# Add and RMS norm over 65,536 rows: the 2-row tile moved from last to first, and the last tile moved in pieces

## The chip, the cores and the metric

The kernel runs on one core of one Trainium2 chip. Times are microseconds (us) of the whole program on the device. One execution at a time was profiled; its page and its trace are what is read below. The profile's span is about 2 us shorter than the measured time of the same execution (3736.0 against 3738.2 for the kernel before); spans are compared with spans and times with times.

## The reference

```python
def setup_inputs():
    batch, seq, dim = 32, 2048, 2048
    return {"x": randn(batch, seq, dim), "residual": randn(batch, seq, dim),
            "gamma": np.ones(dim), "eps": np.float32(1e-6)}        # all float32

def reference(x, residual, gamma, eps):
    z = x + residual
    rms = np.sqrt(np.mean(z ** 2, axis=-1, keepdims=True) + eps)
    return (z / rms * gamma).astype(np.float32)
```

There are 65,536 rows of 2048 floats. Two such arrays are read and one is written, 1610.6 MB together, and each value is used once. Little can be saved by computing faster if the transfers fill the time.

## The kernel before

A tile is 128 partitions times R = 6 rows, 6.29 MB. 65,536 rows are 85 full tiles and one of 2 rows. There are three slots for z (which holds x, then the sum, then the result) and one slot for the residual.

```python
    R = 6
    NZ = 3
    sizes = [R] * n_full + ([left] if left else [])       # 85 x 6 rows, then 2 rows
    ...
    def load_x(i):
        nc.sync.dma_start(out=z_slots[i % NZ][:, : sizes[i], :], in_=rows(x_f, i))
    def load_r(i):
        nc.sync.dma_start(out=r_slot[:, : sizes[i], :], in_=rows(r_f, i))
    def store(i):
        nc.sync.dma_start(out=rows(o_f, i), in_=z_slots[i % NZ][:, : sizes[i], :])

    def compute(i):
        z = z_slots[i % NZ]
        groups = [(a, min(a + 3, sizes[i])) for a in range(0, sizes[i], 3)]
        for a, b in groups:
            # DVE: z += r over three rows; ACT: Square with a running sum, row by row; ACT: Sqrt
            ...
        for (a, b), rms in zip(groups, rms_of):
            # DVE: reciprocal, then z * rstd * gamma, row by row
            ...

    load_x(0)
    load_r(0)
    load_gamma()
    load_x(1)
    compute(0)
    load_r(1)
    for i in range(1, n_tiles):
        store(i - 1)
        if i + 1 < n_tiles:
            load_x(i + 1)
        compute(i)
        if i + 1 < n_tiles:
            load_r(i + 1)
    store(n_tiles - 1)
```

All these transfers are issued by SyncE (SP), in this order, and each waits there for its slot. A full tile's store therefore waits for all its scalings, and the next x load stands behind that store. The residual load of tile i+1 waits for the adds of tile i.

## Time and profile before

| | before |
|---|---|
| time, median of 3 runs | 3736.8 us (3736.49 to 3737.15) |
| DVE, ACT busy | 62%, 29% of the span |
| data moved | 1610.83 MB, mean 431 GB/s |
| rate between 100 and 3690 us | 433 GB/s |

These lines are from the page of the kernel before: the engines' busy time, the DMA share and rate in 40 slices, and the DMA queues (packets, MB, share of the 16 engines' time).

```profile
span 3736.0 us, 2707 instructions
DVE 2311.6 (62%) x858; ACT 1078.6 (29%) x1197; POOL 0.2 (0%) x4
DMA  9999999999999999999999999999999999999998
q1 hardware_dynamic: 37152, 1610.63, 99.7%
q14 instruction: 20, 0.16, 0.0%
```

The DMA engines are busy in every slice, and no other engine is near it. The Trainium skill, "DMA: Bandwidth & Descriptors", section "Where 436 GB/s comes from", puts the ceiling of the sixteen ports at 435.2 GB/s; the trace's 433 agrees with that. So the middle of the kernel has no slack, and what can be won lies at the start and at the end.

The windows view of the kernel before shows the holes. Its columns are the stretch, its length, busy time (and instructions) of DVE, ACT and POOL, the clock, the DMA share and GB/s.

```profile
46.00:48.00 2.00, 0.72 (x2) 1.97 (x5) 0.00 (x0) 1.00 1.07 320
48.00:50.00 2.00, 1.97 (x2) 1.97 (x3) 0.00 (x0) 1.00 0.33 123
76.00:78.00 2.00, 1.97 (x3) 1.90 (x4) 0.00 (x0) 1.00 0.43 147
100.00:3690.00 3590.00, 2220.04 (x821) 1034.05 (x1148) 0.00 (x0) 1.00 1.00 433
3702.00:3714.00 12.00, 11.96 (x7) 4.46 (x7) 0.00 (x0) 1.00 0.13 55
```

The timeline of the kernel before says what the holes waited for: start, duration, engine, line and operation; SPq lines are transfers being issued.

```profile
46.58 0.33 SPq L66 DMA_DIRECT2D r_slot<-in_residual_dram  x1
61.94 0.35 SPq L69 DMA_DIRECT2D out_dram<-z  x1
3693.68 0.33 SPq L66 DMA_DIRECT2D r_slot<-in_residual_dram  x1
3707.33 6.88 DVE L98 SCALAR_TENSOR_TENSOR z<-z,rstd,gamma_tile 128x2048 f32<-128x2048 f32 x3
3714.12 4.41 DVE L76 TENSOR_TENSOR z<-z,r_slot 128x4096 f32<-128x4096 f32 x1
3714.23 13.92 SPq L69 DMA_DIRECT2D out_dram<-z  x2
```

The second residual's load is issued at 46.58, when the three loads before it have drained. At the end the 2-row residual is loaded (from 3693.68, landed on the slowest engine by 3711.4) before the last full tile's scalings end at 3714.2; its store can't go out earlier, and nothing else is queued.

One more thing can be read from the trace. Every transfer is spread over the sixteen DMA engines, and each engine reports when its share has landed. Sorting these sixteen times of one transfer shows how far the engines stand apart. In the kernel before, the last full x or r transfers have twelve engines within 1.1 us, and four late ones: 3.5, 6.8, 7.2 and 9.3 us behind the first. At the start the sixteen lie within 1.7 us.

### The profile page before, as it was taken

What the parts mean: (1) busy time and instruction counts of PE and PEld (TensorE: products, weight loads), DVE (VectorE), ACT (ScalarE), POOL (GpSimd) and SP (SyncE); (2) the same over time, 40 slices, a digit from 0 to 9 for tenths busy, and PEclk for the clock granted to TensorE, in tenths of its full rate; (3) what the DMA queues carried; (4) which work ended last, traced back from release to release, by engine and by line L of the source; (5) the groups of instructions that cost most, each with busy time, mean ns of one, the idle gap of its engine ahead of it and who ended that gap; (6) DMA issues with size and microseconds to landing.
All of it is one profiled execution on the core that took longest, in us unless ns stands there. A gap on an engine that the chain in (4) does not pass through costs nothing.

```text
span 3736.0 us, 2707 instructions
## 1 busy us (share of the span) xinstructions
DVE 2311.6 (62%) x858; ACT 1078.6 (29%) x1197; POOL 0.2 (0%) x4
## 2 busy tenths in 40 slices
DVE  6555666665566666556666655666665566666556
ACT  2222233222223322222332222233222223322223
POOL 0000000000000000000000000000000000000000
DMA  9999999999999999999999999999999999999998
GB/s 410 429 432 434 433 434 432 435 433 434 433 434 433 433 434 434 433 435 432 434 433 434 434 434 433 434 432 435 432 436 432 435 432 435 433 434 433 435 432 369
DMA packets 37180, 1610.83 MB, mean 431 GB/s; under 512 B 4132, under 2 KB 4132, under 8 KB 4132
## 3 DMA queue, kind: packets, MB, share of 16 engines
q1 hardware_dynamic: 37152, 1610.63, 99.7%
q14 instruction: 20, 0.16, 0.0%
q10 hardware_dynamic: 8, 0.03, 0.0%
HBM read 1073.77 MB, written 536.87 MB: 431 GB/s over the span
## 4 chain that ended last, share of the span: by engine, by line
DMA 70%; DVE 30%; issue 0%; ACT 0%; DVEq 0%; SPq 0%
DMA r_slot<-in_residual_dram 70%; DVE z L76 30%; DVE z L98 0%; ACT sq_junk L79 0%; DVE rstd L96 0%; DVEq L160 0%; DVEq L76 0%; SPq L63 0%; ACT rms L86 0%
## 5 line engine op out<-in xcount | busy, mean ns | idle before, releaser
L76 DVE TENSOR_TENSOR z<-z,r_slot 128x6144 f32<-128x6144 f32 x171 | 1111.7, 6542 | 1385.4 <-DMA r_slot<-in_residual_dram 1385.4
L79 ACT ACTIVATE sq_junk<-z 128x2048 f32<-128x2048 f32 x512 | 963.5, 1882 | 2620.0 <-DVE z L76 2603.5
L98 DVE SCALAR_TENSOR_TENSOR z<-z,rstd,gamma_tile 128x2048 f32<-128x2048 f32 x512 | 1173.6, 2347 | 6.0
L79 ACT ACTIVATION_READ_ACCUMULATOR sq_junk<-z 128x1 f32 x512 | 95.5, 186 | 0.0
L86 ACT ACTIVATE rms<-ssq,eps_tile 128x3 f32<-128x3 f32 x171 | 50.7, 296 | 5.5
L96 DVE RECIPROCAL rstd<-rms 128x3 f32<-128x3 f32 x171 | 29.5, 172 | 5.7 <-ACT rms L86 5.7
L114 DVE LOAD_MASK_SELECT gamma_tile<-gamma_tile x1 | 0.0, 14 | 17.8 <-DMA gamma_tile<-in_gamma_dram 17.8
L79 ACT ACT_TABLE_LOAD x1 | 1.3, 1283 | 18.8 <-DMA z<-in_x_dram 18.8
L114 DVE STREAM_SHUFFLE gamma_tile<-gamma_tile 128x2048 f32<-128x2048 f32 x1 | 2.4, 2418 | 0.0
L109 DVE MEMSET gamma_tile<- 128x2048 f32 x1 | 1.8, 1765 | 0.4 <-issue 0.4
L86 ACT ACT_TABLE_LOAD x1 | 1.3, 1283 | 0.0
L60 DVE MEMSET eps_tile<- 128x1 f32 x1 | 0.1, 59 | 0.8 <-PEq L146 0.8
L146 POOL MEMSET const-bfloat16-1.0<- 128x1 bf16 x1 | 0.1, 101 | 0.0
L146 POOL MEMSET const-uint8-127<- 128x1 uint8 x1 | 0.1, 101 | 0.0
L146 POOL MEMSET const-float32-0.0<- 128x1 f32 x1 | 0.1, 98 | 0.2 <-issue 0.2
L146 POOL MEMSET const-float32-1.0<- 128x1 f32 x1 | 0.1, 98 | 0.0
## 6 DMA issues: line engine op xcount, KB each, us to landing
z<-in_x_dram SPq DMA_DIRECT2D x85, 6144.0 KB, 45.0
r_slot<-in_residual_dram SPq DMA_DIRECT2D x85, 6144.0 KB, 30.4
out_dram<-z SPq DMA_DIRECT2D x85, 6144.0 KB, 30.9
z<-in_x_dram SPq DMA_DIRECT2D x1, 2048.0 KB
r_slot<-in_residual_dram SPq DMA_DIRECT2D x1, 2048.0 KB
out_dram<-z SPq DMA_DIRECT2D x1, 2048.0 KB, 7.3
gamma_tile<-in_gamma_dram ACTq DMA_DIRECT2D x4, 8.0 KB
```

What stands on the lines that cost most here:

```text
L60: nc.vector.memset(eps_tile, float(eps))
L76: nc.vector.tensor_add(out=z[:, a:b, :], in0=z[:, a:b, :], in1=r_slot[:, a:b, :])
L79: nc.scalar.activation(out=sq_junk, in_=z[:, g, :], func=Act.Square, accum_out=ssq[:, g - a : g - a + 1],)
L86: nc.scalar.activation(out=rms[:, : b - a], in_=ssq[:, : b - a], func=Act.Sqrt, bias=eps_tile, scale=inv_d,)
L96: nc.vector.reciprocal(out=rstd[:, : b - a], in_=rms[:, : b - a])
L98: nc.vector.scalar_tensor_tensor(out=z[:, g, :], in0=z[:, g, :], scalar=rstd[:, g - a : g - a + 1], in1=gamma_tile, op0=mult, op1=mult,)
L109: nc.vector.memset(gamma_tile, 0.0)
L114: nc.vector.stream_shuffle(gamma_tile, gamma_tile, [0] * 32)
L146: nc = _bacc.Bacc("TRN2", target_bir_lowering=False, num_devices=1)
```

## The change

The intent: put the 2-row tile first, so that the first store comes early; hold its residual in the third z slot, which is free then, so that the next residual can be queued at once; and move the last tile's residual and result in 2-row pieces, so that its computation hides behind the store of the tile before.

```diff
-    sizes = [R] * n_full + ([left] if left else [])
+    sizes = ([left] if left else []) + [R] * n_full
 ...
-    stats = ctx.enter_context(tc.tile_pool(name="stats", bufs=3))
+    stats = ctx.enter_context(tc.tile_pool(name="stats", bufs=6))
 ...
+    last = n_tiles - 1
+    piece = 2
+
+    def pieces(i):
+        k = sizes[i]
+        return [(a, min(a + piece, k)) for a in range(0, k, piece)] if i == last else [(0, k)]
+
+    def r_of(i):
+        return z_slots[NZ - 1] if i == 0 else r_slot
 ...
     def load_r(i):
-        nc.sync.dma_start(out=r_slot[:, : sizes[i], :], in_=rows(r_f, i))
+        for a, b in pieces(i):
+            nc.sync.dma_start(out=r_of(i)[:, a:b, :], in_=rows(r_f, i)[:, a:b, :])
 
     def store(i):
-        nc.sync.dma_start(out=rows(o_f, i), in_=z_slots[i % NZ][:, : sizes[i], :])
+        for a, b in pieces(i):
+            nc.sync.dma_start(out=rows(o_f, i)[:, a:b, :], in_=z_slots[i % NZ][:, a:b, :])
 ...
     def compute(i):
+        if i == last:
+            before = None
+            for a, b in pieces(i):
+                add(i, a, b)
+                rms = square(i, a, b)
+                if before is not None:
+                    scale(i, *before)
+                before = (a, b, rms)
+            scale(i, *before)
+            return
 ...
     load_x(1)
+    load_r(1)
     compute(0)
-    load_r(1)
```

More of the change, by code (lines that the diff above doesn't have):

```diff
@@ L39 @@
     assert n_full * P * R + left * P == n_rows
-    sizes = [R] * n_full + ([left] if left else [])
+    sizes = ([left] if left else []) + [R] * n_full
+    starts = [0]
+    for k in sizes:
+        starts.append(starts[-1] + P * k)
     n_tiles = len(sizes)
@@ L45, in rows @@
         k = sizes[i]
-        a = i * P * R
+        a = starts[i]
         return t[a : a + P * k, :].rearrange("(p r) m -> p r m", r=k)
@@ L65, in load_r, with add, square, scale @@
     def load_r(i):
-        nc.sync.dma_start(out=r_slot[:, : sizes[i], :], in_=rows(r_f, i))
+        for a, b in pieces(i):
+            nc.sync.dma_start(out=r_of(i)[:, a:b, :], in_=rows(r_f, i)[:, a:b, :])
     def store(i):
-        nc.sync.dma_start(out=rows(o_f, i), in_=z_slots[i % NZ][:, : sizes[i], :])
-    def compute(i):
-        z = z_slots[i % NZ]
+        for a, b in pieces(i):
+            nc.sync.dma_start(out=rows(o_f, i)[:, a:b, :], in_=z_slots[i % NZ][:, a:b, :])
+    def add(i, a, b):
+        z = z_slots[i % NZ]
+        nc.vector.tensor_add(out=z[:, a:b, :], in0=z[:, a:b, :], in1=r_of(i)[:, a:b, :])
+    def square(i, a, b):
+        n = b - a
+        ssq = stats.tile([P, 3], fp32, name="ssq")
+        for g in range(n):
+            nc.scalar.activation(
+                out=sq_junk,
+                in_=z_slots[i % NZ][:, a + g, :],
+                func=Act.Square,
+                accum_out=ssq[:, g : g + 1],
+            )
+        rms = stats.tile([P, 3], fp32, name="rms")
+        nc.scalar.activation(
+            out=rms[:, :n], in_=ssq[:, :n], func=Act.Sqrt, bias=eps_tile, scale=inv_d
+        )
+        return rms
+    def scale(i, a, b, rms):
+        n = b - a
+        rstd = stats.tile([P, 3], fp32, name="rstd")
+        nc.vector.reciprocal(out=rstd[:, :n], in_=rms[:, :n])
+        for g in range(n):
+            row = z_slots[i % NZ][:, a + g, :]
+            nc.vector.scalar_tensor_tensor(
+                out=row,
+                in0=row,
+                scalar=rstd[:, g : g + 1],
+                in1=gamma_tile,
+                op0=mult,
+                op1=mult,
+            )
+    def compute(i):
+        if i == last:
[8 more added lines that the diff above has]
+            return
         groups = [(a, min(a + 3, sizes[i])) for a in range(0, sizes[i], 3)]
@@ L75, in compute @@
         for a, b in groups:
-            nc.vector.tensor_add(out=z[:, a:b, :], in0=z[:, a:b, :], in1=r_slot[:, a:b, :])
-            ssq = stats.tile([P, 3], fp32, name=f"ssq{a}")
-            for g in range(a, b):
-                nc.scalar.activation(
-                    out=sq_junk,
-                    in_=z[:, g, :],
-                    func=Act.Square,
-                    accum_out=ssq[:, g - a : g - a + 1],
-                )
-            rms = stats.tile([P, 3], fp32, name=f"rms{a}")
-            nc.scalar.activation(
-                out=rms[:, : b - a],
-                in_=ssq[:, : b - a],
-                func=Act.Sqrt,
-                bias=eps_tile,
-                scale=inv_d,
-            )
-            rms_of.append(rms)
-        for (a, b), rms in zip(groups, rms_of):
-            rstd = stats.tile([P, 3], fp32, name=f"rstd{a}")
-            nc.vector.reciprocal(out=rstd[:, : b - a], in_=rms[:, : b - a])
-            for g in range(a, b):
-                nc.vector.scalar_tensor_tensor(
-                    out=z[:, g, :],
-                    in0=z[:, g, :],
-                    scalar=rstd[:, g - a : g - a + 1],
-                    in1=gamma_tile,
-                    op0=mult,
-                    op1=mult,
-                )
+            add(i, a, b)
+            rms_of.append(square(i, a, b))
+        for (a, b), rms in zip(groups, rms_of):
+            scale(i, a, b, rms)
     def load_gamma():
@@ L128 @@
             load_r(i + 1)
-    store(n_tiles - 1)
+    store(last)
 _INS = ['x', 'residual', 'gamma', 'eps']
```

## The prediction

> **What bounds it.** The DMA engines. The page gives 1610.83 MB and a DMA share of 9 (90% or more) in every slice but the last; DVE is busy 62%, ACT 29%. In the windows view 100 to 3690 us moves 433 GB/s at share 1.00. The Trainium skill, "DMA: Bandwidth & Descriptors", section "Where 436 GB/s comes from", gives a ceiling of 435.2 GB/s for the sixteen ports; this trace agrees to 0.5% (its claim there that HBM binds at about 358 does not fit). A full tile moves 18.87 MB, about 43.5 us; DVE needs about 27.3 us of it. Only time in which DMA stands empty can be won: start and end.
>
> **Start.** In the timeline the second residual load is issued at 46.58, after both adds of tile 0, while the three queued loads have drained; the windows show 123 GB/s in 48:50. The store of tile 0 is issued at 61.94, again about as the queue drains: 147 GB/s in 76:78. Against 433 GB/s the two holes (46:52 at 319, 74:80 at 352) are about 1.6 + 1.1 us.
> After: four loads are queued at once, 16.8 MB, about 39 us plus the slow first packets (x0 landed at about 17.5 to 19 us instead of 16.5), so DMA has work until about 42. The 2-row tile needs: loads landed about 12 to 13, add 4.4 (now ahead of the shuffle), two squares 4.1, table load and Sqrt 1.6, scaling 4.9; even with gamma as late as now (20.8) plus shuffle 2.4 its store is issued by about 30. Both holes go. Worth 2 to 2.7 us.
>
> **End.** The 2-row residual's load is issued at 3693.68 and landed by 3711.4; the store of tile 84 can only be issued at 3714.23, so 3702:3714 moves 55 GB/s. The last store is issued at 3727.8 and lands in 7.3 us, of which 4.9 are transfer (8 packets of 0.612 us per engine).
> But the hole is smaller than it looks: the sixteen engines have drifted apart. Completion records of one DMA spread over 1.7 us at the start and 9.4 us at the end, so late engines still worked until 3711.4. The slowest engine decides the end. It has 8.4 MB in stores after 3711.4: 14.5 + 4.9 = 19.4 us, plus 0.7 to the end: 3731.5 instead of 3736.0.
> After: last tile's pieces of 2 rows: first piece lands 20 us after the previous adds; store 84 (14.5 us) then covers add 4.4, squares 4.4, scaling 4.9 of the pieces; stores are issued about 9.5 us apart, first about 48 us and third about 62 us after r84 landed, where the slowest engine reaches them at 58 and 68. No hole there. Six more 2-row transfers cost 0.34 us (3 x 0.612 against 1.815 us per 48 KB). Worth about 4 us.
>
> **Sum.** 2.2 + 4.0 = 6.2 us off 3736.8: **3730.6 us**, range 3727.5 to 3733.5. Faster by over 2%: 0.005; within 2%: 0.99; slower: 0.005.
>
> **What would show it.** Windows near 433 GB/s from about 5 us with no hole near 46:52 or 74:80; first store issued before 32 us; no stretch under 300 GB/s between 3650 and about 3720 but a slope at the very end of up to 10 us as engines finish one after the other; middle still 433; DVE and ACT sums unchanged.
>
> **What would make it wrong.** The engines' drift being larger or smaller (the end slope costs one for one); fast engines waiting for late stores; the piece chain on DVE and ACT ending after the queue drains; small packets slower than 0.612 us.

## The result, and the profile after

Measured together: 3736.98 us before (4 runs, 3736.49 to 3737.32) and 3728.51 us after (4 runs, 3727.87 to 3729.28), 8.5 us less. The ratio of after to before is 0.9978 with a 95% interval of 0.996 to 0.9995. A ratio here is the mean time of one kernel's fast runs over the mean of the other's fast runs of the same rounds, so it is not quite the ratio of the medians quoted. By the record's threshold of 2% the two count as the same; their ranges lie far apart, so the difference is real but small. In a later session the same two kernels stood 10.1 us apart (3738.08 and 3727.94).

The page after, the same lines:

```profile
span 3726.4 us, 2716 instructions
DVE 2312.2 (62%) x860; ACT 1079.1 (29%) x1198; POOL 0.2 (0%) x4
DMA  9999999999999999999999999999999999999999
q1 hardware_dynamic: 37728, 1610.63, 100.0%
q14 instruction: 20, 0.16, 0.0%
```

The windows view after. The holes at the start are gone, the middle is at 433 as before, and the end slopes off instead of stopping and starting again.

```profile
46.00:48.00 2.00, 2.00 (x1) 0.00 (x0) 0.00 (x0) 1.00 1.37 590
48.00:50.00 2.00, 2.00 (x1) 0.00 (x0) 0.00 (x0) 1.00 0.95 410
76.00:78.00 2.00, 0.00 (x0) 0.00 (x0) 0.00 (x0) 1.00 1.08 467
100.00:3690.00 3590.00, 2226.80 (x824) 1034.10 (x1148) 0.00 (x0) 1.00 1.00 433
3700.00:3710.00 10.00, 9.93 (x7) 4.74 (x8) 0.00 (x0) 1.00 0.84 360
3710.00:3718.00 8.00, 4.58 (x2) 0.00 (x0) 0.00 (x0) 1.00 0.95 403
3718.00:3722.00 4.00, 0.00 (x0) 0.00 (x0) 0.00 (x0) 1.00 0.73 311
3722.00:3726.00 4.00, 0.00 (x0) 0.00 (x0) 0.00 (x0) 1.00 0.11 45
```

(The rate of one 2 us window can exceed the ceiling, because a packet's bytes are all counted in one window; read neighbours together.)

The timeline after: the first store is issued at 29.41, the three pieces of the last residual from 3659.45, the store of the tile before the last and the three pieces of the last result from 3680.00 on.

```profile
14.43 4.43 DVE L89 TENSOR_TENSOR z<-z,z 128x4096 f32<-128x4096 f32 x1 [11.40 <-DMA z<-in_residual_dram]
29.41 0.35 SPq L85 DMA_DIRECT2D out_dram<-z  x1
3659.45 7.27 SPq L81 DMA_DIRECT2D r_slot<-in_residual_dram  x3
3680.00 34.93 SPq L85 DMA_DIRECT2D out_dram<-z  x4
```

Where did the 9.6 us between the two spans come from? The mean rate can't tell, because it is 433 in the middle of both. What ends the program is the slowest of sixteen engines. So I made a ledger from the completion records: for a point in the work given in MB moved, the landing time minus the time which the fastest engines need for that much (14.505 us per 6.29 MB, measured in the middle). The number is the delay accumulated so far, in us. It was made for all kernels that move the data in the same large pieces (the other kernels are described under the experiments):

| kernel | at 63 MB: mean of 16 engines | at 63 MB: slowest | at 1573 MB: mean | at 1573 MB: slowest |
|---|---|---|---|---|
| before | 7.9 | 9.1 | 10.2 | 17.5 |
| before, run again | 8.1 | 9.8 | 10.5 | 18.2 |
| third slot alone (head_only) | 7.5 | 8.0 | 10.1 | 15.6 |
| end alone (tail_only) | 7.8 | 9.5 | 10.3 | 15.6 |
| after | 4.6 | 6.8 | 7.3 | 12.3 |
| after, run again | 4.5 | 7.1 | 6.9 | 12.2 |
| short tile first, own slot (own_slot) | 4.5 | 6.7 | 7.0 | 12.1 |
| short tile first, uncut end (whole_last) | 4.4 | 6.6 | 6.8 | 12.7 |

From before to after the slowest engine gained 2.3 us by 63 MB (9.1 to 6.8), a further 2.9 us by 1573 MB (17.5 to 12.3 is 5.2 in all), and the remaining 9.6 - 5.2 = 4.4 us at the end. The mean engine gained 3.3 us at the start and then nothing more (2.9 at 1573 MB). The prediction had 2.2 at the start, nothing in the middle and 4.0 at the end.

The table also shows how much of this is the luck of the profiled execution. The profiled time minus the slowest engine's number at 1573 MB is 3720.6 to 3720.7 us in the three traces with the uncut end (before, before again, head_only), 3716.0 in after, after again and own_slot, and 3715.8 in tail_only. So the slowest engine alone sets the time, to about 0.1 us. Worked out from these constants, an execution at the median stands at 16.3 (kernel before, 3736.98 us) and 12.5 (kernel after, 3728.51 us) in the last column. Of the 8.5 us measured, about 2.3 then belong to the start, 1.5 to the middle and 4.7 to the end (an estimate). The experiments ask whether the parts are what they seem, and what the middle part is.

### The profile page after: what moved, and what is told of

Same layout as the page of the kernel before. It is cut to its first block, busy times and chain, and to the rows that moved or that the text cites. A ratio compares the mean times of both kernels' runs of the same rounds, so it can differ in the third digit from the quotient of the medians.

```text
span 3726.4 us, 2716 instructions
## 1 busy us (share of the span) xinstructions
DVE 2312.2 (62%) x860; ACT 1079.1 (29%) x1198; POOL 0.2 (0%) x4
## 4 chain that ended last, share of the span: by engine, by line
DMA 69%; DVE 30%; issue 0%; DVEq 0%; SPq 0%
DMA r_slot<-in_residual_dram 69%; DVE z L89 30%; DVE z L113 0%; DVE rstd L110 0%; DVEq L194 0%; DVEq L89 0%; SPq L77 0%; SPq L81 0%
## 5 line engine op out<-in xcount | busy, mean ns | idle before, releaser
L89 DVE TENSOR_TENSOR z<-z,r_slot 128x6144 f32<-128x6144 f32 (+1 forms) x171 | 1107.6, 6517 | 1380.4 <-DMA r_slot<-in_residual_dram 1380.4
L102 ACT ACTIVATE rms<-ssq,eps_tile 128x3 f32<-128x3 f32 (+1 forms) x172 | 51.0, 296 | 5.5
L110 DVE RECIPROCAL rstd<-rms 128x3 f32<-128x3 f32 (+1 forms) x172 | 29.7, 172 | 3.3 <-ACT rms L102 3.2
L143 DVE MEMSET gamma_tile<- 128x2048 f32 x1 | 1.8, 1765 | 0.4 <-issue 0.4
```

Source lines behind the costliest of these rows:

```text
L89: nc.vector.tensor_add(out=z[:, a:b, :], in0=z[:, a:b, :], in1=r_of(i)[:, a:b, :])
L102: nc.scalar.activation(out=rms[:, :n], in_=ssq[:, :n], func=Act.Sqrt, bias=eps_tile, scale=inv_d)
L110: nc.vector.reciprocal(out=rstd[:, :n], in_=rms[:, :n])
L143: nc.vector.memset(gamma_tile, 0.0)
```

## The experiments

Ten experiments were run (two of them are the two kernels again), five executions each, all correct, in three sessions, each on another chip of the machine. The kernel before ran in each session nine times: 3738.08 us (3736.29 to 3738.85) in the first, 3737.15 (3736.19 to 3737.71) in the second, 3736.98 (3735.72 to 3739.07) in the third. So a difference between two sessions is safe to about 1 us, and differences of less are not read.

| kernel | median us | range of 5 runs | ratio to before, 95% interval |
|---|---|---|---|
| before_again | 3737.79 | 3736.19 to 3738.88 | 1.0, 0.9987 to 1.0012 |
| after_again | 3727.94 | 3727.89 to 3728.84 | 0.9974, 0.9961 to 0.9986 |
| own_slot | 3728.23 | 3728.08 to 3729.34 | 0.9975, 0.9961 to 0.9988 |
| mid_tile | 3741.20 | 3740.50 to 3741.67 | 1.0008, 0.9996 to 1.0021 |
| head_only | 3736.53 | 3736.08 to 3737.56 | 0.9999, 0.9986 to 1.0013 |
| tail_only | 3732.44 | 3731.43 to 3733.11 | 0.9988, 0.9975 to 1.0 |
| whole_last | 3743.51 | 3742.96 to 3743.71 | 1.0017, 1.0005 to 1.003 |
| pad72 | 3763.73 | 3763.23 to 3764.85 | 1.0072, 1.006 to 1.0085 |
| pad12_act | 3733.00 | 3732.86 to 3734.00 | 0.9989, 0.9977 to 1.0002 |
| pad12_pool | 3729.26 | 3728.70 to 3731.15 | 0.998, 0.9966 to 0.9993 |

The intervals are wide beside such differences, and some reach 1.0; where a difference from the kernel before is read below, the ranges of the executions of the same session do not overlap (tail_only and mid_tile, for instance), or it is said that it is within the noise.

### Both kernels again

No edit. The question was whether the distance between the engines belongs to the kernel or to one execution.

> The kernel before, unchanged, to see whether the drift of the sixteen DMA engines is a property of the kernel or of one execution. If of the kernel: the completions of one of the last full transfers spread over 9 to 10 us again (9.4 before), each jump of about 0.7 us at an instruction fetch. If it is chance: spread anywhere from 6 to 12 us, and the profiled span moves with it. Time 3737 either way.

> The changed kernel, unchanged. If the drift belongs to the kernel: spread 7.0 to 7.6 us near the end again (7.3 before), time 8 to 9 us below the kernel before. If chance: another spread, and the gain lies between 6.5 and 9 us, moving with the spread.

The late engines near the end stood at 2.7, 7.2, 8.3 and 10.0 us behind the first in the kernel before (6.8, 7.2 and 9.3 were the last three the first time), and at 4.3, 5.8, 7.0 and 7.7 in the kernel after (4.1, 5.5, 7.1, 7.3). So each kernel repeats itself to about 1 us. The kernel before is the less steady: the fourteen runs of its code in that session span 2.7 us, the five of the kernel after 1 us.

### The third slot: not needed, and not enough

own_slot is the changed kernel with the third slot taken back:

```diff
     def r_of(i):
-        return z_slots[NZ - 1] if i == 0 else r_slot
+        return r_slot
 ...
-    load_r(1)
     compute(0)
+    load_r(1)
```

> The 2-row tile still goes first, but its residual goes into the residual slot and tile 1's residual is loaded only after tile 0's add. Theory: the short tile alone closes the hole at the start, because x0, r0 and x1 (10.5 MB) keep DMA busy to about 28 us while tile 0's add ends at about 19; time within 1 us of the changed kernel. Rival (the third slot is what closes it): a hole of 2 us or more between 19 and 32 us and 2 to 3 us more time.

It took 3728.23 us against 3727.94 for the changed kernel in the same session. The second residual's load was issued at 18.89, as soon as the short tile's add was done. The windows view of own_slot has no hole around it:

```profile
18.00:30.00 12.00, 8.00 (x6) 5.58 (x6) 0.00 (x0) 1.00 0.97 422
30.00:46.00 16.00, 0.92 (x1) 0.00 (x0) 0.00 (x0) 1.00 0.98 403
```

head_only is the kernel before with the third slot as the only change:

```diff
+    def r_of(i):
+        return z_slots[NZ - 1] if i == 0 else r_slot
 ...
     load_x(1)
+    load_r(1)
     compute(0)
-    load_r(1)
```

> The kernel before with one thing alone: the residual of its six-row first tile goes into the third z slot, so that the second residual's load need not wait for tile 0's adds. Theory: no gain. The hole at 46 to 50 goes, but the store of tile 0 is still issued at about 62 while the queue now drains at about 61 instead of 63, so the same 2 to 3 us of emptiness come back at 61 to 64; time within 1 us of the kernel before. Rival (the third slot closes the hole): 2 to 3 us faster, no stretch under 300 GB/s before 70 us.

It took 3736.53 us, 0.6 less than before, which is inside the noise. The windows view of head_only shows the hole moved, not closed. At 46 to 50 all is full now, and at 60 to 62 it is empty, because the first store is still issued only at 62.07:

```profile
46.00:48.00 2.00, 0.72 (x2) 1.97 (x5) 0.00 (x0) 1.00 1.20 516
48.00:50.00 2.00, 1.96 (x2) 1.97 (x3) 0.00 (x0) 1.00 1.02 442
60.00:62.00 2.00, 2.00 (x1) 0.00 (x0) 0.00 (x0) 1.00 0.12 49
```

Together the two runs settle the start: the short first tile does it, since it brings both the add (18.8 instead of 46.6) and the first store (29.4 instead of 61.9) far ahead of the moment at which the queue drains. The third slot is neither necessary nor sufficient.

### The end alone

tail_only leaves order and start as in the kernel before. The last full tile's store goes out in two halves, and the 2-row tile is computed and stored row by row:

```diff
     def store(i):
-        nc.sync.dma_start(out=rows(o_f, i), in_=z_slots[i % NZ][:, : sizes[i], :])
+        step = 1 if i == n_tiles - 1 else 3 if i == n_tiles - 2 else R
+        for a in range(0, sizes[i], step):
+            b = min(a + step, sizes[i])
+            nc.sync.dma_start(out=rows(o_f, i)[:, a:b, :], in_=z_slots[i % NZ][:, a:b, :])
 ...
-        groups = [(a, min(a + 3, sizes[i])) for a in range(0, sizes[i], 3)]
+        step = 1 if i == n_tiles - 1 else 3
+        groups = [(a, min(a + step, sizes[i])) for a in range(0, sizes[i], step)]
```

> The kernel before with only its end changed, the 2-row tile left last: the last full tile's store goes out in two three-row halves, the 2-row tile is computed and stored row by row. Theory: the first half's store is issued 20 us after its residual landed, 7 us earlier than now and before the slowest engine runs dry (24 us), so the 12 us hole before the end goes and 4 to 4.5 us are gained (3733.5); the start keeps its holes and the slowest engines are still 9 to 10 us behind near the end. Rival (the gain at the end needs the short tile moved away): less than 2 us gained.

It took 3732.44 us, 4.7 less than the kernel before of the same session (expected 4 to 4.5). The trace of tail_only has the first half issued at 3705.31, while late engines still worked, and the long hole is not there:

```profile
3700.00:3710.00 10.00, 9.96 (x7) 4.53 (x7) 0.00 (x0) 1.00 0.74 318
3710.00:3714.00 4.00, 4.00 (x3) 0.00 (x0) 0.00 (x0) 1.00 0.92 393
```

So the end is worth 4 to 5 us, with or without moving the tile. The expected lateness of 9 to 10 us was a miss: the slowest engine stood 7.4 us behind here, and 7.7 in head_only.

### Moving the tile without cutting the last one

whole_last is the changed kernel with `last = n_tiles`, so that no tile is cut.

```diff
-    last = n_tiles - 1
+    last = n_tiles  # no tile is cut
 ...
-    store(last)
+    store(n_tiles - 1)
```

> The changed kernel without the cutting: 2-row tile first, last six-row tile loaded, computed and stored whole. Theory: the last store can be issued only 27 us after its residual landed and takes 14.5 us more, where the pieces end about 29 us after r85 landed: about 14 to 15 us slower than the changed kernel, 5 to 7 us slower than the kernel before. So moving the tile without cutting loses.

It took 3743.51 us: 15.6 more than the changed kernel of the session before, 6.4 more than the kernel before, both close to what was expected. The windows of whole_last show 14 us with no transfer at all while DVE finishes the last tile, and then its store on its own:

```profile
3710.00:3724.00 14.00, 13.90 (x8) 6.23 (x7) 0.00 (x0) 1.00 0.00 0
3724.00:3740.00 16.00, 0.00 (x0) 0.00 (x0) 0.00 (x0) 1.00 0.91 393
```

The move needs the cut: a 2-row tile at the end was a cheap way to end, and its removal has to be paid for by cutting. The cut does not need the move, as tail_only showed.

### A design that went wrong: the short tile in the middle

mid_tile was meant to isolate the end by putting the 2-row tile out of the way, at place 40, with the last tile in pieces.

```diff
-    sizes = ([left] if left else []) + [R] * n_full
+    sizes = [R] * 40 + ([left] if left else []) + [R] * (n_full - 40)
```

(and the third slot taken back as in own_slot.)

> Only the end is changed: six-row tile first and residual as in the kernel before, the 2-row tile at place 40, last tile in pieces. If end and start add up as in the ledger of the two traces (end 4.4 us, start 2 to 3, drift of the slowest engine 2 to 3): hole of 2 to 3 us at 46 to 52 and the slow stretch at 74 to 80 are there again, tail as in the changed kernel, time 2 to 3 us above the changed kernel and about 5 to 6 below the kernel before if the drift is chance; 4.4 below it, with spread 9.4, if the drift comes from the start.

It took 3741.20 us, 3.1 more than the kernel before, where less was expected. The windows of mid_tile show why:

```profile
1744.00:1746.00 2.00, 1.97 (x3) 0.00 (x0) 0.00 (x0) 1.00 0.27 115
1746.00:1748.00 2.00, 2.00 (x2) 0.00 (x0) 0.00 (x0) 1.00 0.08 33
1748.00:1750.00 2.00, 2.00 (x2) 0.00 (x0) 0.00 (x0) 1.00 0.00 0
1750.00:1752.00 2.00, 2.00 (x2) 0.00 (x0) 0.00 (x0) 1.00 0.00 0
```

A short tile has short loads, but the store of the tile before it comes as late as ever (issued at 1751.59). The hole at the end of the kernel before was this same hole; I had moved it to the middle and overlooked it. A short tile leaves the queue short wherever a full tile precedes it. First is the one place where none does. The hole also brought the engines back into step: 5.4 us apart before it, 0.8 after it, and only 6.0 at the end.

### What sets the engines apart

The steps in the lag of the late engines lie at the moments of the instruction fetches (q14). The Trainium skill, "Runtime: NRT & Kernel Launch", section "Instruction fetch mechanics", says that each engine's sequencer drives its own DMA queue to fetch the next instructions while the current ones run, and calls the cost mostly hidden. In these traces a fetch is one packet of 8 KB that takes 0.309 us on one DMA engine. To test whether these packets set the DMA engines apart, tiny instructions were added that move no data. pad72 is the changed kernel with this, after each six-row tile but the last:

```diff
         for (a, b), rms in zip(groups, rms_of):
             scale(i, a, b, rms)
+        if i > 0:
+            for _ in range(72):
+                nc.scalar.activation(out=pad_a, in_=rms_of[-1][:, :1], func=Act.Square)
```

> The changed kernel with 72 tiny activations on one element added after each six-row tile but the last, on ACT, which has the time for them (about 18 us of 31 idle per tile). They move no data, but add 6048 instructions, so about 47 more instruction fetches of 8 KB on the instruction queue (20 now). If each fetch sets one DMA engine back by about 0.7 us: the sum of all engines' lags grows by about 33 us (2 us on the mean), the slowest engine lags 10 us or more instead of 7.3, time 2 to 6 us longer. Rival (fetches are not the cause): time within 1 us of the changed kernel, lags as in it.

It took 3763.73 us, 35 us more than the changed kernel (3728.5 and 3727.9). The rival fell, and my own figure of 2 to 6 was far too small. The lines of pad72's page and groups: 67 instruction packets instead of 20, and the added instructions took 0.203 us each, which ACT had to spare. They did not lengthen the chain of computation either: in this kernel as in the changed one a full tile's store was issued 27.2 us after its residual had landed, in all 84 tiles.

```profile
q14 instruction: 67, 0.55, 0.0%
L143 ACT ACTIVATE pad_a<-rms 128x1 f32<-128x1 f32 x6048 | 1226.5, 203 | 191.3
```

The windows of pad72 show when it began to cost:

```profile
100.00:1000.00 900.00, 546.84 (x203) 557.47 (x1786) 0.00 (x0) 1.00 1.00 433
1000.00:2000.00 1000.00, 621.92 (x230) 619.88 (x1949) 0.00 (x0) 1.00 1.00 429
2000.00:3000.00 1000.00, 611.37 (x225) 614.38 (x1932) 0.00 (x0) 1.00 1.00 429
```

The completion records explain both. One engine, always the slowest, fell back by about 0.69 us at each of ACT's fetches: its lag went from 6.87 us (at 671 us) to 7.56 (at 715, after a fetch at 710) to 8.25 (at 773, after one at 769). I had spread the fetches over the engines; they all went to one. 47 more fetches times 0.69 us are 32 us, close to the 35 measured. Up to about 1300 us the other fifteen engines went on at 433 GB/s. When the slow one was some 14 us behind, the others began to wait for it, and everything ran at its pace. 14 us is about what the order of transfers allows. There is one residual slot, so the next residual's load is issued only 13.1 us after the residual before it has landed on the slowest engine (2014.89 to 2028.04 in pad72), and its packets start about 1.9 us later. Until then a fast engine has one store and one x load to work on, 2 x 14.5 = 29.0 us. So an engine that is more than 29.0 - 13.1 - 1.9 = 14.0 us ahead finds its queue empty (an estimate from the records of pad72). The completions agree that the wait is there: from 1500 us on a residual took the fast engines 15.0 us instead of 14.5, while stores and x loads stayed at 14.5.

The last pair asks whether it matters whose instructions are fetched. pad12_act is pad72 with 12 instead of 72. pad12_pool has the same 1008 instructions on POOL:

```diff
+            for _ in range(12):
+                nc.gpsimd.tensor_copy(out=pad_a, in_=rms_of[-1][:, :1])
```

> The changed kernel with 12 tiny activations after each six-row tile but the last, on ACT: 1008 more instructions there, so 8 more fetches of 8 KB. In the run with 72 each ACT fetch set one and the same DMA engine, the slowest, back by 0.69 us. If fetches of one engine's instructions always burden one DMA engine and that one becomes or stays the slowest: its lag grows from 7.3 to about 12.5 to 13 us, time 5 to 5.5 us longer than the changed kernel (3733.5). It stays below the about 14 us at which the other engines began to wait. Rival (small instructions cost by their own time on ACT): no lag grows, no change, or a change seen in ACT waits on the chain.

> The same 1008 tiny instructions on POOL, which has 4 now. The same number of fetches, but for another engine's instructions. Theory: they burden another DMA engine, which was not among the late ones, by 8 x 0.69 = 5.5 us, which stays below the 7.3 us of the slowest: time within 1 us of the changed kernel, and one more late engine near 5.5 us in the completions. Rival (any fetch costs all alike): 5 us longer as with ACT.

The instruction queues of pad12_act and of pad12_pool (20 packets in the changed kernel):

```profile
q14 instruction: 28, 0.23, 0.0%
q14 instruction: 31, 0.25, 0.0%
```

Lag of the last six engines behind the first, in us, in one of the last transfers at about 3645 us:

```
after        1.8  3.8  4.1  5.5  7.1  7.3
pad12_act    2.7  3.5  4.4  5.3  7.1 12.5
pad12_pool   3.3  4.2  5.6  5.9  6.7  8.6
```

pad12_act took 3733.00 us, about 4.5 to 5 more than the changed kernel (3728.51 and 3727.94 in other sessions). Exactly one engine went from about 7.3 to 12.5 us, and the others stayed: 5.2 us for 8 more fetches (28 instead of 20 packets), 0.65 us each. pad12_pool, with 31 packets, took 3729.26 us, 0.7 to 1.3 more than the changed kernel. One engine more stands among the late ones, and the slowest is 1.3 us later than in the changed kernel, which is about what the time shows. The difference of about 1 us from the changed kernel is no more than two sessions can differ by; the 3.7 us between the two padded kernels are from one session. So the same number of tiny instructions costs about 5 us on ACT, whose fetches meet an engine that is already among the slowest, and about 1 on POOL, whose fetches meet another one. (The records give times and no engine numbers, so which of the late engines in the last row is POOL's can't be said.)

## Why the prediction was right or wrong

**The time, 3730.6 us with 3727.5 to 3733.5: held by the measured 3728.51, and the sign and the order of the gain were right.** The gain was 8.5 us where 6.2 was forecast, 10.1 in a later session.

**What bounds the kernel: right.** 433 GB/s in the middle of both kernels, and DVE and ACT sums unchanged (2311.6 to 2312.2, 1078.6 to 1079.1).

**The end, "about 4 us": right in mechanism and size.** 4.4 us in the ledger, 4.7 us in tail_only, which changed the end alone. The chain of the pieces ran as forecast: the first and third piece of the result were issued 48.0 and 61.7 us after the residual of the tile before had landed (3652.86 to 3700.82 and 3714.60), where 48 and 62 had been expected. The reasoning that the 12 us hole is worth only about 4, because late engines still worked until 3711.4, was the step that mattered; counting the hole at its full length would have forecast some 10 us. The six further small transfers at 0.34 us in all were too small to be told apart; a 16 KB packet took 0.611 us as before.

**The start, "2 to 2.7 us", used as 2.2: right in mechanism, undersized.** The ledger has 2.3 us for the slowest engine by 63 MB, but 3.3 us for the mean engine. Two holes in the windows view were counted, at 46:52 and 74:80. Part of the loss is not emptiness. Packets of 48 KB take 1.815 us in the middle; in the kernel before, those beginning at 45 to 50, at 75 to 80 and at 105 to 110 us took up to 3.4, 3.0 and 2.7 us, which adds 0.74, 1.01 and 0.70 us for each engine. The third spell lies in no hole, and I had not looked for it. After the change such packets add only about 0.8 us, around 40 us. Both kernels have one more, of 0.8 to 0.9 us, in their first 5 us. The spells came where all or most of the engines were within about 1.5 us of each other and the direction of the transfers changed or a queue started anew; later, when the engines stand apart, hardly any packet is slow. mid_tile supports this: when its hole had brought the engines from 5.4 to 0.8 us apart, two spells of 0.95 and 0.81 us came back (1765 to 1770 and 1795 to 1800 us). But there, too, the queue had just started anew, so that being in step is the cause is argued, not shown.

**"Both holes go": right, but the credit was put partly in the wrong place.** The prediction began with four loads queued at once. own_slot queues three and is as fast; head_only queues four and gains nothing.

**"Middle still 433": right for the mean and wrong for what matters.** This is the step that failed. The sum took the lag of the slowest engine from the kernel before (9.4 us) and carried it over, so it had no term for the middle; a larger or smaller drift stood only among the things that would make it wrong. In the kernel after the lag is 7.3, and between the two traces the slowest engine gained 2.9 us more in the middle, where nothing had been changed. The mean of the sixteen engines lost the same there in both (2.3 and 2.7 us between 63 and 1573 MB); what differs is how the losses fall on single engines. The pads show one mechanism: each instruction fetch sets one DMA engine back by 0.65 to 0.69 us, all of ACT's fetches fall on the same DMA engine, and while the queue does not run empty nothing is made up.

What the runs do not settle is why the kernel before loads its slowest engine more. The four traces that begin with a full tile ended with 15.6 to 18.2 in the ledger, the four that begin with the short tile with 12.1 to 12.7. In each of these eight traces one engine also loses steadily between fetches, 0.9 to 1.3 us per 1000 us (read between 2380 and 2740 us). In the two traces of the kernel before this engine is the slowest of all, 4.3 and 5.0 us behind the fast ones already at 886 us; in the six others it comes from further ahead and ends third from last, at 5.3 to 6.1 us. tail_only has the start of the kernel before unchanged and is among the six, so the place of this engine is at least in part luck: both profiled executions of the kernel before were slow ones of their kind (3738.16 and 3738.88 us), and that of tail_only (3731.43 us) was the fastest of its five. At the medians the middle is worth about 1.5 us instead of 2.9 (the estimate above). Why an engine loses steadily, and what sets its place at the start, stays open.

None of the other kernels beats the changed one. own_slot equals it with simpler code.

## What to carry to other kernels

When DMA bounds a kernel, look at the sixteen engines one by one, since the slowest one ends the program and the mean rate hides it; a hole is worth only what it costs the slowest engine, so read the completion times before counting its length. Put an odd short tile first, where no full tile's store stands before it, and cut the last full tile so that its work hides behind the store before it. Here the move without the cut lost 6.4 us and the short tile in the middle lost 3.1, while cutting the end alone won 4.7. In this kernel instructions cost transfer time even on an engine with time to spare (1008 tiny ones about 5 us on ACT, about 1 on POOL), so in such a kernel drop small instructions, or try them on another engine.

## What the Trainium skill lacked or had wrong

- "DMA: Bandwidth & Descriptors", section "Where 436 GB/s comes from", says that for transfers between HBM and SBUF the HBM side binds at about 358 GB/s. Every large transfer here has HBM at one end, and 433 GB/s were held for 3590 us on one core. The ceiling of 435.2 GB/s in the same section fits. A note further up the page has about 358 only for two cores of a pair that stream at once, which no run here shows; the section itself does not say so.
- "Runtime: NRT & Kernel Launch", section "Instruction fetch mechanics", speaks of refills in blocks of 16 KiB (256 instructions) whose cost is mostly hidden. The records show packets of 8 KB, about one for 128 added instructions (47 more for 6048). They are hidden from the computing engine, but each cost a DMA engine 0.65 to 0.69 us, more than twice the packet's own 0.309 us; 6048 tiny instructions on an engine with time to spare made this kernel 35 us longer. That all of ACT's fetches burden one DMA engine is on neither of these two pages.
- "DMA: Bandwidth & Descriptors", section "Latency and other measured facts", says that DMA engines 7 and 15 are usually slower and offers, as a guess, a cause that belongs to transfers issued from GpSimd. No transfer here was issued from there, and three engines still fell 5.5 to 10 us behind over 3.7 ms, in part at instruction fetches. (The completion records don't number the engines.)
- No page read speaks of packets slowing down in spells while the sixteen engines stand close together: up to 3.4 us instead of 1.815 us for 48 KB in the first 110 us, and hardly any later. The cause is not shown.
